# A two-layer transformer with a modulated conv and attention block on one core: five small moves in a hand-written order of work

## The chip, the core and the metric

The kernel runs on one core of a Trainium2 chip. The metric is the time of one execution in microseconds on the device (us). Before the change the median of three runs is 2548.13 us, from 2547.11 to 2549.5.

## What is computed

The input x has 256 positions of width 2048, all in float32. Two transformer layers come first, the first with stick-breaking attention, the second with latent attention; each ends in `residual_update`, where `x + rms_norm(out)` gets a gated term. Then one modulated block follows. Cut to what matters here:

```python
def residual_update(x, out, g_post, p_i, w_pp, w_pg):
    x = x + rms_norm(out, g_post)
    return x + (p_i @ w_pp) * jax.nn.sigmoid(x @ w_pg)
...
mod = silu(c) @ w_ada + b_ada                       # 2048 -> 6 * 2048
sh1, sc1, gt1, sh2, sc2, gt2 = split(mod, 6)
h = rms_norm_2(x, g_pre_mix) * (1.0 + sc1) + sh1
u_glu, q, k, v, qi, ki, wi, gates = split(h @ w_in)
y_conv = silu(layer_norm(depthwise_conv_31_taps(a * sigmoid(gt)))) @ w_conv_out
y_attn = top_64_attention(q, k, v, qi, ki, wi) @ w_attn_out
mixed = (g_conv * y_conv + g_attn * y_attn) @ w_o
x = x + gt1 * rms_norm_2(mixed, g_post_mix)
h = rms_norm_2(x, g_pre_ffn) * (1.0 + sc2) + sh2
x = x + gt2 * rms_norm_2((silu(h @ w_gate) * (h @ w_up)) @ w_down, g_post_ffn)
```

The convolution runs over 1024 channels with 31 taps each along the positions.

## The kernel before

**Products.** The 256 positions are two tiles t of 128. Each float32 product is made of three products of a high and a low part: for each 128 rows of a weight, L270 multiplies the left side's high part with the weight's high part wh, L271 the high part with the weight's low part wl, and L272 the low part with wh. The usual form is 128x512 (weight slices of 512 columns; 384 and smaller occur too).

**Units and blocks.** A block is one 512-wide column slice of a weight matrix, times both tiles. `Run.go` goes through the blocks in order. Its smallest step is a unit u: one tile t and one weight item i (two chunks of 128 rows for a 512-wide slice, so six matmuls). `self.u` counts the units, and everything else is placed by this counter when the program is written; the engines then run their instructions in that order, each engine for itself.

**Weights.** `pump` brings weights up to LEAD = 10 units ahead of use. `load` (L131) sends a transfer from the SP queue into a staging tile `wst`, of which there are STAGE = 4. `consume` makes wh with ACT (L148) and wl with DVE (L149) from it, into rings of RING = 6 tiles; weights with a gain use L153 and L154.

**Side work.** Whatever is not a main product is written as generators, which `side` advances once per unit; `yield n` means that the next step comes n units later. Those added by `add` are the urgent ones. `ensure` forces the generators that a product's left side still lacks. When tile 0 of a block with an `enter` function is written (a phase change), `go` first finishes all urgent generators and then calls `enter` (L277 to L280).

**Modulation.** The 6 x 2048 values of `mod` are made in 24 column pieces q of 512, each from 16 chunks k. A chunk is a transfer of 256 KB issued by POOL (L247) into a tile `ast` (XBUF = 3) and one DVE row (L416 for k = 0, otherwise L419), which adds it into `ada` with the value of silu(c) as the scalar. `spread` gives each chunk a unit; pieces 0 to 19 lie between unit 100 and unit uf − 60 (uf is the first FFN unit), without the surroundings of phase changes, and pause for the start of the modulated block. `side` writes either one chunk's DVE row or one chunk's transfer in a unit. After chunk 15, `ada_sum(q)` is added: a high part on ACT (L432), a low part on DVE (L433), two matmuls with a matrix of ones (L436, L437) that sum over the partitions, twice; a store to `mod`; and after each fourth piece a load back and a transpose on PE (L452). For `gt1` and `gt2` a row of gates is made and stored as well. `gain_of` (DVE) turns `sc` into the gain of a norm, and `begin_m` broadcasts the gate row at the phase change to w_o.

**Out projections.** After the output product of a layer, `to_gate` updates x (DVE L786) and transposes it (PE L370, called by `feed`), as the left side of the gate product. `feed` makes the transposed tile's high part (`ah`, ACT L381, or in its very first call DVE L379) and low part (`al`, DVE L383; without a scale DVE L375).

**Convolution.** `conv` makes one group of 128 channels: a first row (DVE L1234) and 30 rows (DVE L1237), which add one tap each on 128 partitions with up to 255 positions. After four rows or so it yields CONV_PACE units. `conv_chain` runs through channel groups 0 to 3 and 4 to 7, and then `conv_norm`. At the same time, DVE makes the scores and the top-64 selection of the attention (L1358 to L1375), and the weight splits.

ACT loads a table of functions (ACT_TABLE_LOAD) wherever its function is not in the loaded one.

Of the kernel before, what the change touches and what calls it, by code (L numbers as in the profile page):

```python
# [31 lines left out]
AHEAD_F = 3  # L32
LEAD_AHEAD = 20
LEAD_TURN = 6
CONV_PACE = 3
TO_C = ((2, 2, 2, (0, 2)), (2, 2, 2, (0, 2)))
TO_F = ((2, 2, 2, (0, 1, 2)), (2, 4, 2, (0, 1, 2)))
G_AT = (-1, -1, -1, 7)
# [51 lines left out]
class Run:  # L90
# [3 lines left out]
    def __init__(self, nc, main, psum, blocks, extra):  # L94
        self.nc, self.main, self.psum, self.blocks = nc, main, psum, blocks
        self.u = 0
        self.freed = 0
        self.urgent = []
        self.queue = deque()
        self.active = []  # L100
        self.width, self.space, self.last = 2, 4, -100
        self.items, self.need, u = [], [], 0
        for b in blocks:
            b.items = [{"p": len(self.items) + i, "b": b, "i": i} for i in range(b.np)]
            b.u0 = u
            first = {}
            for t, i in b.units():
                first.setdefault(i, u)
                u += 1
            self.items += b.items  # L110
            self.need += [first[i] for i in range(b.np)]
        self.ring = [0]
        for it in self.items:
            it["ahead"] = it["i"] < it["b"].n_ahead
            self.ring.append(self.ring[-1] + (not it["ahead"]))
        self.nextc = self.nextd = 0
        self.hooks = {}
        self.extra = extra(self) if extra else []
        self.xd = self.xc = 0
# [60 lines left out]
    def add(self, gen, act=None, t=None):  # L180
# [3 lines left out]
            act.gens[t].append(rec)  # L184
        return rec

    def back(self, gen, after=(), acts=()):
        rec = [gen, 0, False, after]
        self.queue.append(rec)
        for act, t in acts:  # L190
            act.gens[t].append(rec)
        return rec
# [34 lines left out]
    def side(self):  # L227
        for rec in list(self.urgent):
            if not rec[2] and rec[1] <= self.u:
                self.advance(rec)  # L230
        self.urgent = [r for r in self.urgent if not r[2]]
        self.active = [r for r in self.active if not r[2]]
        if (self.queue and len(self.active) < self.width and self.u >= self.last + self.space
                and all(r[2] for r in self.queue[0][3])):
            rec = self.queue.popleft()
            rec[1] = self.u
            self.active.append(rec)
            self.last = self.u
        self.step()
        if self.xc < self.xd and self.extra[self.xc][0] <= self.u:  # L240
            x = self.extra[self.xc]
            x[2](x[3])
            self.xc += 1
        elif (self.xd < len(self.extra) and self.xd - self.xc < XBUF and self.extra[self.xd][0] - 12 <= self.u):
            x = self.extra[self.xd]
            st = self.main.tile([P, NB], F32, tag="ast", bufs=XBUF, name="ast")
            self.nc.gpsimd.dma_start(st, x[1])  # L247
            x.append(st)
            self.xd += 1

    def go(self):
        nc = self.nc
        for b in self.blocks:
# [4 lines left out]
            for t, i in b.units():  # L258
                if t not in acc:
                    tag, bufs = ("sc", 2) if b.spare and t == 1 else ("acc", 3)  # L260
                    acc[t] = self.psum.tile([P, NB], F32, tag=tag, bufs=bufs, name=tag)
                it = b.items[i]
                self.ensure(act, t, b.cp * (i + 1))
                self.pump(it["p"])
                wh, wl = it["w"]
# [17 lines left out]
                    self.advance(rec)  # L283
                self.side()
                self.pump()
        while self.urgent or self.queue or self.active:
            self.u += 1
            self.side()

# [2 lines left out]
def body(ctx, tc, a, out):  # L292
# [68 lines left out]
        x.part = lambda t, g, m: tuple(y[:, g : g + m, sl(t)] for y in tiles())  # L361
        return x

    def feed(act, t, kc0, src, scale=None, first=False):


        m = src.shape[-1] // P
        tp = psum_t()
# [6 lines left out]
            nc.vector.tensor_sub(lo, v, hi.bitcast(F32))  # L375
        else:
            for c in range(m):
                if first:
                    nc.vector.tensor_scalar(hi[:, c, :], v[:, c, :], scale(kc0 + c), None, op0=ALU.mult)  # L379
                else:  # L380
                    nc.scalar.activation(hi[:, c, :], v[:, c, :], AF.Copy, scale=scale(kc0 + c))  # L381
            for c in range(m):
                nc.vector.scalar_tensor_tensor(lo[:, c, :], v[:, c, :], scale(kc0 + c), hi[:, c, :].bitcast(F32),  # L383
                                               op0=ALU.mult, op1=ALU.subtract)
# [24 lines left out]
    def ada_chunk(q, k):  # L409
        c0 = q * NB  # L410

        def use(w):
# [5 lines left out]
            acc = ada_acc[q]  # L418
            nc.vector.scalar_tensor_tensor(acc, w, s, acc, op0=ALU.mult, op1=ALU.add)  # L419
            if k == 15:  # L420
                run.add(ada_sum(q))

        return a["w_ada_2"][0, k * P : (k + 1) * P, c0 : c0 + NB], use

# [42 lines left out]
            yield 3  # L467
            st["gp"] = row_tile(gate_row(1))

    mod_rows, gate_rows = {}, {}  # L470

    def gate_row(n):
        return gate_rows[n].rearrange("(o k) p -> o (k p)", o=1)
# [1 line left out]
    def mod(i):  # L475
        return mods[:, 16 * i : 16 * i + 16]
# [53 lines left out]
    def begin_a():  # L530
# [47 lines left out]
        def prep():  # L578
            for g in range(4):
                for t in range(2):  # L580
                    feed(actA, t, 4 * g, x_nat[t][:, g * NB : (g + 1) * NB], lambda k: pre0[:, k : k + 1],
                         first=g == 0 and t == 0)
                    if g == 0 and t == 0:
                        warm(2)
                    yield PREP[2 * g + t]
# [252 lines left out]
    def layer_tail(layer, w_out, act_o, src, act_gate, act_next, then, last_groups=None):  # L838
# [13 lines left out]
                run.add(f(), act_p, t)  # L852

        def to_gate(t, r, update):
            yield 2
            xs = [update(0)]
            yield 1
            for g in range(4):
# [306 lines left out]

    def gain_of(i, name):

        nc.vector.scalar_tensor_tensor(gsc[:, i, :], mod(3 * i + 1), 1.0, cols[:, GC[name] : GC[name] + 16],
                                       op0=ALU.add, op1=ALU.mult)

# [365 lines left out]
        nc.scalar.activation(xo, xo, AF.Copy, accum_out=st["oss"][t][:, 4 + j : 5 + j])  # L1536

    def begin_m():
        st["gp"] = row_tile(gate_row(0))

    out_phase(a["w_o_2"][0], actM, begin_m, lambda t: spill[1][t], actF, to_f, mix_sums, last_groups=[1, 1, 6])
# [89 lines left out]
    def spread(run):  # L1631
# [3 lines left out]
        turns = [b.u0 for b in blocks if b.enter is not None or b.ahead is not None or b.w.tensor.name == a["w_ple_proj"].tensor.name]  # L1635
        xs = []
        uc = conv_block.u0
        for qs, us in ((range(20), calm(100, uc - 30) + calm(uc + 290, uf - 60)), (range(20, 24), calm(uf + 40, uf + 300))):
            todo = [(q, k) for q in qs for k in range(16)]
            for i, (q, k) in enumerate(todo):  # L1640
                xs.append([us[len(us) * i // len(todo)], *ada_chunk(q, k)])
# [53 lines left out]
```

## Time and profile before

| what | value |
|---|---|
| median of 3 runs | 2548.13 us (2547.11 to 2549.5) |
| profiled execution, its own time | 2550.05 us |
| span of the profile | 2548.3 us |
| mean clock granted to the matmuls in it | 0.992 |
| DMA | 562.49 MB, mean 221 GB/s |
| chain that ended last | PE 89%, DVE 4%, ACT 3%, DMA 2%, issue 1%, POOL 1% |

The span runs from the first to the last instruction of the profile; the execution's own time is 1.75 us longer. Engines are PE (matmul), PEld (its weight loads), DVE (vector), ACT (activation), POOL and SP. A row of a timeline shows the start, the duration, the engine, the line of the kernel, the operation, the output and inputs, the count and, in brackets, how long the engine was idle before and what ended that. Matmuls are pipelined: a 128x512 matmul has 0.39 us, but the next one starts earlier, so distances between starts are what counts. PEclk is the granted clock, 1.00 at full speed.

### The profile page before, as it was taken

Reading aid. Unit: us, or ns where it says so; the run is one execution under the profiler, and the core shown is the slowest. Engines: PE = TensorE matmul, PEld = TensorE weight load, DVE = VectorE, ACT = ScalarE, POOL = GpSimd, SP = SyncE. Lnnn points to the kernel's source line nnn. Section 1 sums busy time; section 2 is a strip of 40 time slices with the busy share of each in tenths; the row PEclk is TensorE's granted clock in tenths of the full one; section 3 lists DMA queues with packets and bytes.
Section 4 is the critical chain, followed back from the end, with each engine's and each line's share of the span. In section 5 each row is a group of like instructions: output and inputs, shape, how many; then the busy total and the mean of one; then the engine's idle time right before and its main releaser. Section 6 shows DMA issues by size and latency. Waiting matters only on the chain.

```text
span 2548.3 us, 33086 instructions
## 1 busy us (share of the span) xinstructions
PE 2489.3 (98%) x11904; PEld 2066.6 (81%) x11904; DVE 1708.6 (67%) x2349; ACT 1298.0 (51%) x1915; POOL 298.2 (12%) x561
## 2 busy tenths in 40 slices
PE   9999999999999999999999999989999999999998
PEld 7888888778888777878877878877788888888886
DVE  5466677777865577667998857775765566655545
ACT  6655564556656545554544564445544444444443
POOL 2011112211324321000000001110110010000000
PEclk9999999999999999999999999999999999999999
DMA  7577778877885496665647547884577777676563
GB/s 243 177 235 254 254 229 304 276 231 251 286 256 169 156 325 225 220 201 177 189 141 209 176 135 256 288 281 164 184 240 235 238 236 235 219 236 189 190 193 125
DMA packets 272212, 562.49 MB, mean 221 GB/s; under 512 B 20985, under 2 KB 43929, under 8 KB 270001
## 3 DMA queue, kind: packets, MB, share of 16 engines
q1 hardware_dynamic: 236688, 438.56, 54.5%
q0 software_dynamic: 34448, 120.67, 13.7%
q8 instruction: 93, 1.52, 0.2%
q10 hardware_dynamic: 912, 1.17, 0.1%
q14 instruction: 71, 0.57, 0.1%
HBM read 551.86 MB, written 8.45 MB: 220 GB/s over the span
## 4 chain that ended last, share of the span: by engine, by line
PE 89%; DVE 4%; ACT 3%; DMA 2%; issue 1%; POOL 1%; DVEq 0%; SPq 0%; ACTq 0%; POOLq 0%
PE acc L270 20%; PE acc L272 20%; PE acc L271 20%; PE sc L270 7%; PE sc L272 7%; PE sc L271 7%; DVE wl L149 1%; PE sc L1049 1%; PE tp L370 1%; ACT wh L148 1%; PE pv L1049 1%; DMA ast<-in_w_ada_dram 1%; DMA wst<-in_w_o_dram 0%; PE sc L677 0%; DVE cv L1237 0%
## 5 line engine op out<-in xcount | busy, mean ns | idle before, releaser
L149 DVE TENSOR_TENSOR wl<-wst,wh 128x1024 fp32r<-128x1024 f32 (+3 forms) x794 | 948.8, 1199 | 578.8 <-ACT wh L148 576.5
L148 ACT ACTIVATE wh<-wst 128x1024 fp32r<-128x1024 f32 (+3 forms) x794 | 822.3, 1039 | 829.8 <-PE sc L272 421.9
L270 PE MATMUL acc<-wh,ah 128*128 128x512 f32 (+4 forms) x1918 | 752.1, 392 | 3.0 <-ACT wide L1441 3.0
L271 PE MATMUL acc<-wl,ah 128*128 128x512 f32 (+4 forms) x1918 | 738.9, 385 | 1.5 <-DVE wl L149 1.5
L272 PE MATMUL acc<-wh,al 128*128 128x512 f32 (+4 forms) x1918 | 738.4, 385 | 0.9 <-DVE al L375 0.9
L270 PEld LDWEIGHTS acc<-wh,ah 128*128 128x128 f32 x1918 | 362.6, 189 | 72.4 <-ACT wide L1441 3.4
L272 PEld LDWEIGHTS acc<-wh,al 128*128 128x128 f32 x1918 | 361.9, 189 | 72.6 <-DVE al L375 1.4
L271 PEld LDWEIGHTS acc<-wl,ah 128*128 128x128 f32 x1918 | 362.7, 189 | 67.7 <-DVE wl L149 3.3
L247 POOL DMA_DIRECT2D ast<-in_w_ada_dram x384 | 209.1, 545 | 1553.8 <-DVE ada L419 1298.0
L419 DVE SCALAR_TENSOR_TENSOR ada<-ast,silu_c,ada 128x512 f32<-128x512 f32 x360 | 269.5, 749 | 60.1 <-DMA ast<-in_w_ada_dram 59.6
L270 PE MATMUL sc<-wh,ah 128*128 128x512 f32 x554 | 218.8, 395 | 0.0
L271 PE MATMUL sc<-wl,ah 128*128 128x512 f32 x554 | 216.9, 391 | 0.0
L272 PE MATMUL sc<-wh,al 128*128 128x512 f32 x554 | 216.8, 391 | 0.0
L272 PEld LDWEIGHTS sc<-wh,al 128*128 128x128 f32 x554 | 104.7, 189 | 22.3
L271 PEld LDWEIGHTS sc<-wl,ah 128*128 128x128 f32 x554 | 104.8, 189 | 21.2
L270 PEld LDWEIGHTS sc<-wh,ah 128*128 128x128 f32 x554 | 104.5, 189 | 21.0
L1237 DVE SCALAR_TENSOR_TENSOR cv<-cv,wdw 128x255 f32<-128x255 f32 (+14 forms) x240 | 112.3, 468 | 6.5
L153 ACT ACTIVATE wh<-wst,cols 128x512 fp32r<-128x512 f32 (+2 forms) x112 | 68.3, 666 | 33.3 <-PE acc L272 20.1
L154 DVE SCALAR_TENSOR_TENSOR wl<-wst,cols,wh 128x512 fp32r<-128x512 f32 (+2 forms) x112 | 71.7, 684 | 17.7 <-ACT wh L153 17.5
L270 PE MATMUL sc<-wh,hh 128*128 128x512 f32 x176 | 68.9, 392 | 0.0
L270 PE MATMUL acc<-wh,hh 128*128 128x512 f32 x176 | 68.9, 391 | 0.0
L272 PE MATMUL sc<-wh,hl 128*128 128x512 f32 x176 | 68.6, 390 | 0.0
(377 smaller groups left out, 2887.0 us busy)
## 6 DMA issues: line engine op xcount, KB each, us to landing
ast<-in_w_ada_dram POOLq DMA_DIRECT2D x384, 256.0 KB, 4.3
wst<-in_w_in_dram SPq DMA_DIRECT2D x144, 512.0 KB
wst<-in_w_in_a_dram SPq DMA_DIRECT2D x120, 512.0 KB
wst<-in_w_gate_dram SPq DMA_DIRECT2D x88, 512.0 KB
wst<-in_w_up_dram SPq DMA_DIRECT2D x88, 512.0 KB
wst<-in_w_down_dram SPq DMA_DIRECT2D x88, 512.0 KB
wst<-in_w_ple_gate_dram SPq DMA_DIRECT2D x64, 512.0 KB
wst<-in_w_in_b_dram SPq DMA_DIRECT2D x40, 512.0 KB
```

The source lines that it names most:

```text
L148: nc.scalar.activation(wh, st, AF.Copy)
L149: nc.vector.tensor_sub(wl, st, wh.bitcast(F32))
L153: nc.scalar.activation(wh[:, c, :], st[:, c, :], AF.Copy, scale=g)
L154: nc.vector.scalar_tensor_tensor(wl[:, c, :], st[:, c, :], g, wh[:, c, :].bitcast(F32), op0=ALU.mult, op1=ALU.subtract)
L247: self.nc.gpsimd.dma_start(st, x[1])
L270: nc.tensor.matmul(o, lhsT=hi, rhs=wh[:, c, :], start=kc == 0, stop=False)
L271: nc.tensor.matmul(o, lhsT=hi, rhs=wl[:, c, :], start=False, stop=False)
L272: nc.tensor.matmul(o, lhsT=lo, rhs=wh[:, c, :], start=False, stop=kc == b.cp * b.np - 1)
L370: nc.tensor.transpose(tp[:, c * P : (c + 1) * P], src[:, c * P : (c + 1) * P], ident)
L419: nc.vector.scalar_tensor_tensor(acc, w, s, acc, op0=ALU.mult, op1=ALU.add)
L1049: nc.tensor.matmul(o, lhsT=l, rhs=r, start=start, stop=True, skip_group_check=True)
L1237: nc.vector.scalar_tensor_tensor(acc[:, sft:], u[:, : S - sft], wdw[:, c, k : k + 1], acc[:, sft:], op0=ALU.mult, op1=ALU.add)
```

## The change

It has five parts.

1. `ada_sum` is no longer an urgent generator but goes on a list `slow`, which `side` advances after the urgent ones and which a phase change does not finish. `ready` finishes the sums that a user needs, in `gain_of` and `begin_m`. Pieces 0 to 19 are spread up to unit uf − 110 instead of uf − 60.
2. `to_gate` waits four units instead of two before its first update, in both layers.
3. In the first block, the weights of a unit are pumped ahead of the generators for its left side.
4. The first feed no longer makes its high parts on DVE; all are made on ACT.
5. CONV_PACE is 2 instead of 3.

```diff
-CONV_PACE = 3
+CONV_PACE = 2
...
+    def later(self, gen):
+
+        rec = [gen, self.u + 1, False]
+        self.slow.append(rec)
+        return rec
...
-        self.urgent = [r for r in self.urgent if not r[2]]
-        self.active = [r for r in self.active if not r[2]]
+        for rec in self.slow:
+            if rec[1] <= self.u:
+                self.advance(rec)
+        self.urgent, self.slow, self.active = ([r for r in x if not r[2]] for x in (self.urgent, self.slow, self.active))
...
                 it = b.items[i]
+                if b is self.blocks[0]:
+                    self.pump(it["p"])
                 self.ensure(act, t, b.cp * (i + 1))
                 self.pump(it["p"])
...
-                if first:
-                    nc.vector.tensor_scalar(hi[:, c, :], v[:, c, :], scale(kc0 + c), None, op0=ALU.mult)
-                else:
-                    nc.scalar.activation(hi[:, c, :], v[:, c, :], AF.Copy, scale=scale(kc0 + c))
+                nc.scalar.activation(hi[:, c, :], v[:, c, :], AF.Copy, scale=scale(kc0 + c))
...
-                run.add(ada_sum(q))
+                ada_done.setdefault(q // 4, []).append(run.later(ada_sum(q)))
...
+    def ready(*vectors):
+        for i in vectors:
+            for rec in ada_done[i]:
+                run.finish(rec)
...
         def to_gate(t, r, update):
-            yield 2
+            yield 4
...
     def gain_of(i, name):
+        ready(3 * i, 3 * i + 1)
...
     def begin_m():
+        ready(2)
         st["gp"] = row_tile(gate_row(0))
...
-calm(uc + 290, uf - 60)
+calm(uc + 290, uf - 110)
```

The order of the instructions on the engines shows where they come to stand. Line numbers of the changed kernel are some 6 to 12 higher: L280 to L282 are its three products, L1248 its conv row, L1386 its end of the selection. First DVE, behind the end of the top-64 selection (`sel`), where the convolution (`cv`) of the kernel before begins its sixth group of channels:

```order
L1375 TENSOR_SCALAR sel<-score 128x384
L149 TENSOR_TENSOR wl<-wst,wh 128x1024
L1234 TENSOR_SCALAR cv<-cv,wdw,cols 128x256
L1237 SCALAR_TENSOR_TENSOR cv<-cv,wdw 128x255
L1237 SCALAR_TENSOR_TENSOR cv<-cv,wdw 128x254
L149 TENSOR_TENSOR wl<-wst,wh 128x1024
L1237 SCALAR_TENSOR_TENSOR cv<-cv,wdw 128x253
L1237 SCALAR_TENSOR_TENSOR cv<-cv,wdw 128x252
L1237 SCALAR_TENSOR_TENSOR cv<-cv,wdw 128x251
L1237 SCALAR_TENSOR_TENSOR cv<-cv,wdw 128x250
L149 TENSOR_TENSOR wl<-wst,wh 128x1024 x2
```

The same place of the changed kernel, where the eighth and last group is half done:

```order
L1386 TENSOR_SCALAR sel<-score 128x384
L149 TENSOR_TENSOR wl<-wst,wh 128x1024
L1248 SCALAR_TENSOR_TENSOR cv<-cv,wdw 128x241
L1248 SCALAR_TENSOR_TENSOR cv<-cv,wdw 128x240
L1248 SCALAR_TENSOR_TENSOR cv<-cv,wdw 128x239
L1248 SCALAR_TENSOR_TENSOR cv<-cv,wdw 128x238
L149 TENSOR_TENSOR wl<-wst,wh 128x1024
L1248 SCALAR_TENSOR_TENSOR cv<-cv,wdw 128x237
L1248 SCALAR_TENSOR_TENSOR cv<-cv,wdw 128x236
L1248 SCALAR_TENSOR_TENSOR cv<-cv,wdw 128x235
L1248 SCALAR_TENSOR_TENSOR cv<-cv,wdw 128x234
L149 TENSOR_TENSOR wl<-wst,wh 128x1024
```

Before, 6 channel groups have been begun at this place; now all 8, so more conv rows stand ahead of the same weight split, and four of them lie between any two splits.

PE at the phase change to w_o before, with the sums' matmuls (`adh`, `adl`, `ada`) between two products:

```order
L270 MATMUL acc<-wh,ah 128x512
L271 MATMUL acc<-wl,ah 128x512
L272 MATMUL acc<-wh,al 128x512
L436 MATMUL tp<-adh,ones_r 128x256
L437 MATMUL tp<-adl,ones_r 128x256
L436 MATMUL tp<-adh,ones_r 128x256
L437 MATMUL tp<-adl,ones_r 128x256
L452 MATMUL tp<-ident,ada 128x16
L270 MATMUL sc<-wh,ah 128x512
```

PE of the changed kernel where its last transpose of these sums stands, about a hundred matmuls earlier:

```order
L280 MATMUL acc<-wh,cv 128x512
L281 MATMUL acc<-wl,cv 128x512
L282 MATMUL acc<-wh,cv 128x512
L458 MATMUL tp<-ident,ada 128x16
L280 MATMUL acc<-wh,cv 128x512
L281 MATMUL acc<-wl,cv 128x512
```

The transpose, and with it the four matmuls ahead of it, have left the phase change and stand among the product before w_o.

ACT at the start of the program before (`wh` the weights' high parts, `ah` those of the first feeds):

```order
L148 ACT_TABLE_LOAD
L148 ACTIVATE wh<-wst 128x512 x4
L381 ACTIVATE ah<-tp,pre_77 128x128 x8
L148 ACTIVATE wh<-wst 128x512 x3
L381 ACTIVATE ah<-tp,pre_77 128x128 x4
```

And in the changed kernel:

```order
L148 ACT_TABLE_LOAD
L148 ACTIVATE wh<-wst 128x512 x4
L387 ACTIVATE ah<-tp,pre_77 128x128 x12
L148 ACTIVATE wh<-wst 128x512 x3
L387 ACTIVATE ah<-tp,pre_77 128x128 x4
```

Four high parts have come from DVE to ACT, behind the first four weight copies.

More of the change, by code (lines that the diff above doesn't have):

```diff
@@ L97, in __init__ @@
         self.freed = 0
-        self.urgent = []
+        self.urgent, self.slow = [], []
         self.queue = deque()
@@ L285, in go @@
                 self.pump()
-        while self.urgent or self.queue or self.active:
+        while self.urgent or self.queue or self.active or self.slow:
             self.u += 1
@@ L362, in pair_act, with feed @@
         return x
-    def feed(act, t, kc0, src, scale=None, first=False):
+    def feed(act, t, kc0, src, scale=None):
         m = src.shape[-1] // P
@@ L468, in ada_sum @@
             st["gp"] = row_tile(gate_row(1))
-    mod_rows, gate_rows = {}, {}
+    mod_rows, gate_rows, ada_done = {}, {}, {}
+    def ready(*vectors):
+        for i in vectors:
+            for rec in ada_done[i]:
+                run.finish(rec)
     def gate_row(n):
@@ L580, in prep @@
                 for t in range(2):
-                    feed(actA, t, 4 * g, x_nat[t][:, g * NB : (g + 1) * NB], lambda k: pre0[:, k : k + 1],
-                         first=g == 0 and t == 0)
+                    feed(actA, t, 4 * g, x_nat[t][:, g * NB : (g + 1) * NB], lambda k: pre0[:, k : k + 1])
                     if g == 0 and t == 0:
@@ L1637, in spread @@
         uc = conv_block.u0
-        for qs, us in ((range(20), calm(100, uc - 30) + calm(uc + 290, uf - 60)), (range(20, 24), calm(uf + 40, uf + 300))):
+        for qs, us in ((range(20), calm(100, uc - 30) + calm(uc + 290, uf - 110)), (range(20, 24), calm(uf + 40, uf + 300))):
             todo = [(q, k) for q in qs for k in range(16)]
```

## The prediction

> **What bounds the kernel now.** I read the page first, then the waits of PE, then busy time stretch by stretch where the diff touches something, then timelines of the single waits.
>
> ```profile
> span 2548.3 us, 33086 instructions
> ...
> PE 2489.3 (98%) x11904; PEld 2066.6 (81%) x11904; DVE 1708.6 (67%) x2349; ACT 1298.0 (51%) x1915; POOL 298.2 (12%) x561
> ```
>
> PE is busy for 98% of the span. An edit can shorten the run only by PE's waits and slow-clock stretches, and lengthens it wherever it makes PE wait. The waits of PE name the places (us in total, times, longest):
>
> ```profile
> PE tp L370 <- DVE x L786: 6.1, 6, 2.0
> PE tp L452 <- DMA ada<-mod: 4.1, 1, 4.1
> PE tp L436 <- ACT adh L432: 3.7, 3, 2.2
> ...
> PE acc L270 <- ACT wide L1441: 3.0, 1, 3.0
> ...
> PE tp L370 <- issue: 2.5, 1, 2.5
> PE tp L437 <- DVE adl L433: 2.5, 3, 0.9
> PE acc L271 <- DVE wl L149: 1.5, 1, 1.5
> ```
>
> L436, L437 and L452 are the modulation sums (10.3 us together), L370 the transposes after the residual update. DVE's weight split L149 stops PE once, at the start. Now the busy time of all engines, in the convolution, just after it, in the w_o phase change and behind it, and in two pieces of layer 0's residual update (columns: PE, PEld, DVE, ACT, POOL, then the granted clock and DMA):
>
> ```profile
> 1158.00:1344.00 186.00, 186.00 (x943) 158.41 (x943) 168.50 (x322) 85.83 (x118) 0.00 (x0) 1.00 0.57 168
> 1349.00:1356.00 7.00, 6.95 (x19) 5.47 (x20) 6.79 (x12) 2.60 (x4) 0.00 (x0) 0.58 0.71 220
> 1722.00:1729.00 7.00, 6.96 (x21) 5.59 (x22) 2.85 (x5) 4.43 (x11) 0.00 (x0) 0.65 0.00 1
> 503.00:507.00 4.00, 2.66 (x14) 1.82 (x12) 4.00 (x6) 2.36 (x4) 0.00 (x0) 1.00 0.73 251
> 516.00:520.00 4.00, 2.00 (x12) 1.41 (x11) 2.87 (x4) 2.03 (x3) 0.54 (x1) 1.00 0.78 257
> ```
>
> In the 186 us from 1158 to 1344 PE never waits, but DVE has only 186 − 168.5 = 17.5 us of idle time. Elsewhere DVE has room (67% over the span); there it has not. What fills it, the groups of DVE in that stretch:
>
> ```profile
> L1237 DVE SCALAR_TENSOR_TENSOR cv<-cv,wdw 128x255 f32<-128x255 f32 (+9 forms) x164 | 76.9, 469 | 4.5
> L149 DVE TENSOR_TENSOR wl<-wst,wh 128x1024 fp32r<-128x1024 f32 (+2 forms) x67 | 73.9, 1113 | 12.3 <-ACT wh L148 12.2
> ...
> L1234 DVE TENSOR_SCALAR cv<-cv,wdw,cols 128x256 f32<-128x256 f32 x6 | 2.4, 407 | 0.0
> ```
>
> **The denser conv steps.** The convolution is 8 channel groups of 31 rows, 248 DVE rows in all. Before, 164 + 6 = 170 of them lie ahead of 1344 us. With a pace of 2 units instead of 3, the order of the changed kernel puts all 248 ahead of the weight split that stands at 1342.45 here. That split is already just in time (DVE, then PE, then the two ACT groups that PE waits for):
>
> ```profile
> 1342.45 2.35 DVE L149 TENSOR_TENSOR wl<-wst,wh 128x1024 fp32r<-128x1024 f32 x2
> ```
>
> ```profile
> 1344.54 0.39 PE L270 MATMUL acc<-wh,ah 128*128 128x512 f32 x1
> ...
> 1349.05 0.79 PE L270 MATMUL acc<-wh,ah 128*128 128x512 f32 x1 [2.99 <-ACT wide L1441]
> ...
> 1355.06 0.40 PE L272 MATMUL acc<-wh,al 128*128 128x512 f32 x1
> ```
>
> ```profile
> 1347.46 1.06 ACT L148 ACTIVATE wh<-wst 128x1024 fp32r<-128x1024 f32 x1 [2.01 <-DMA wst<-in_w_in_dram]
> 1348.42 1.06 ACT L1441 ACTIVATE wide<-acc 128x512 f32<-128x512 f32 x2
> ```
>
> The first half of the x2 group ends near 1343.7, and the unit that needs it starts at 1344.54: 0.9 us of slack. DVE is in order, so 248 − 170 = 78 more rows at 0.469 us, 36.6 us, stand in front of it. If all 17.5 us of idle time and the slack absorb what they can, PE waits 36.6 − 17.5 − 0.9 = 18.2 us. If the idle time before L149, 12.3 us of waiting for ACT's half, cannot be filled, it is 18.2 + 12.3 = 30.5 us. The fuller DVE is, the less it waits for ACT, so I take a value near the lower end, 21 us. Spread over many units, this should leave the clock alone: from 503 to 507 and from 516 to 520 PE was busy for 66% and 50% of the time at a clock of 1.00. The wait of 2.99 us at 1349.05 was, however, followed by slow matmuls (clock 0.58): the 14 steps from 1349.05 to 1355.06 took 6.01 us, and at 0.227 us each would take 3.2, so 2.8 us went there. Is that stall of 2.99 + 2.8 = 5.8 us still there afterwards? ACT's L1441 stands behind a weight copy that waits for a transfer into a staging tile, and that tile comes free only with a DVE split four items earlier. DVE will be as late then as now, so I leave the stall in; it may go (−5.8), or a second cold stretch may come (+2.8). Conv stage: +21, from 18.2 − 5.8 = +12.4 to 30.5 + 2.8 = +33. After it DVE is freer than before, which returns nothing, as PE does not wait for DVE there.
>
> On the clock the Trainium skill (TensorE: Matmul & The Clock Gate, Part 1: The HAM clock gate) says that the gate watches free-running windows of about 3.4 us and throttles after an idle one. The wait of 2.99 us is shorter and was followed by 0.58 all the same, so the trace bears the rule out only roughly; by the page alone no second cold stretch could come from waits like these, and the upper end would be 30.5 instead of 33.
>
> The order also puts 23 table loads on ACT instead of 18, since exponentials and sigmoids now alternate. A load took 1.28 us:
>
> ```profile
> L1025 ACT ACT_TABLE_LOAD x2 | 2.6, 1283 | 0.0
> ```
>
> Five are 6.4 us. ACT is idle for 100 of the 186 us, so I cost them at nothing; all of them on the path would be +6.4, part of my upper side. The Trainium skill (ScalarE: Activation LUTs, What ACT_TABLE_LOAD costs) adds a drain and gives 2.66 us a switch: an estimate of 13.3 us, which that idle time would hold too.
>
> **Modulation sums that nobody waits for.** PE at the w_o phase change, then at the earlier one:
>
> ```profile
> 1711.13 0.39 PE L271 MATMUL acc<-wl,ah 128*128 128x512 f32 x1
> 1711.36 0.39 PE L272 MATMUL acc<-wh,al 128*128 128x512 f32 x1
> 1712.43 0.38 PE L436 MATMUL tp<-adh,ones_r 128*128 128x256 f32 x1 [0.69 <-ACT adh L432]
> ...
> 1722.05 0.26 PE L452 MATMUL tp<-ident,ada 16*128 16x16 f32 x1 [4.12 <-DMA ada<-mod]
> 1722.23 0.80 PE L270 MATMUL sc<-wh,ah 128*128 128x512 f32 x1
> ...
> 1726.66 0.52 PE L271 MATMUL acc<-wl,ah 128*128 128x512 f32 x1
> ```
>
> ```profile
> 919.32 0.39 PE L272 MATMUL acc<-wh,al 128*128 128x512 f32 x1
> ...
> 922.25 0.39 PE L436 MATMUL tp<-adh,ones_r 128*128 128x256 f32 x1 [0.77 <-ACT adh L432]
> ...
> 922.93 0.40 PE L270 MATMUL acc<-wh,ah 128*128 128x512 f32 x1
> ```
>
> Matmuls start 0.227 us apart (1711.13, 1711.36), so the product could go on at 1711.59; it does at 1722.23, 10.6 us later. The five small matmuls move into the stream and keep some 0.7 us. The 11 steps from 1722.23 to 1726.66 take 4.43 us instead of 2.50: 1.9 more. Saved: 10.6 − 0.7 + 1.9 ≈ 12 us. At the earlier one 922.93 − 919.55 = 3.4, less 0.5 of moved work: 2.9 us. In the new order the last transpose of the sums stands in the product before w_o, about a hundred matmuls ahead, so no guard finds one undone. The gate row's broadcast still starts at this phase change; it is used only by the block's output, so it is covered. Ends: −16 and −10.
>
> **Transposes two units later.** In both layers PE waits at L370 for DVE's residual update, the 6.1 us above, and 2.5 us put down to issue: 8.6 us at most can go. But DVE itself is late there, and partly for a transfer:
>
> ```profile
> 502.25 0.75 DVE L419 SCALAR_TENSOR_TENSOR ada<-ast,silu_c,ada 128x512 f32<-128x512 f32 x1 [1.73 <-DMA ast<-in_w_ada_dram]
> ...
> 517.13 0.75 DVE L419 SCALAR_TENSOR_TENSOR ada<-ast,silu_c,ada 128x512 f32<-128x512 f32 x1 [1.43 <-DMA ast<-in_w_ada_dram]
> ```
>
> ```profile
> 987.88 0.75 DVE L419 SCALAR_TENSOR_TENSOR ada<-ast,silu_c,ada 128x512 f32<-128x512 f32 x1 [3.94 <-DMA ast<-in_w_ada_dram]
> ```
>
> Update and transposes move together, and ending the chunk stream 50 units earlier makes chunks denser, so some more L419 rows (0.66 us apart) come between. I take −1, between −8.6 and +4 (six rows more).
>
> **The start.** The hi halves of the first feed move from DVE, idle then, to ACT behind four weight copies:
>
> ```profile
> 6.28 1.12 DVE L379 TENSOR_SCALAR ah<-tp,pre 128x128 fp32r<-128x128 f32 x4 [2.74 <-PE tp L370]
> ...
> 9.28 0.63 ACT L148 ACTIVATE wh<-wst 128x512 fp32r<-128x512 f32 x1 [0.89 <-DMA wst<-in_w_in_a_dram]
> ...
> 9.68 0.63 PE L272 MATMUL acc<-wh,al 128*128 128x512 f32 x1
> ```
>
> ACT is through with the copies at 9.9 and each half then needs 0.3 us on ACT and as much on DVE, so the first L272 comes near 11 instead of 9.68: +1.5, between 0 (the weights' transfers are late next) and +3 (all four halves in the chain).
>
> **Sum**, on the profiled run's 2550.05 us: + 21 − 12 − 2.9 − 1 + 1.5 = + 6.6, so 2556.7. The median of the runs shown, 2548.13, is 1.9 below the profiled run: 2554.8, rounded to 2555.0.
>
> **Rivals.** All times are against the median; a difference of 0.2%, 5.1 us, is about what a measurement of this kernel can tell from none, so the bounds are 2543.0 and 2553.2.
> - *DVE's lead swallows the conv rows* (faster): DVE splits weights up to ten units ahead of PE (60 matmuls at 0.227, 13.6 us at most), and that lead comes on top of the idle time. Once both together hold more than 30 of the 36.6 us, the conv stage costs 4 us or so, the other terms (−12 − 2.9 − 1 + 1.5 = −14.4) win, and the time is 2548.1 + 4 − 14.4 ≈ 2538. Against it: the lead was there before too, and was used up by 1342. 0.10; and 0.04 for a conv stage at +12 with transposes at −5: 2542.
> - *Gains and losses meet* (same): the conv stage at its low end, +12.4, as the old stall goes: 2548.1 + 12.4 − 14.4 ≈ 2546. For it speaks DVE's lighter load behind the convolution; against it, that the staging tile still waits for a late split. Up to 2553 with the ends between: 0.26.
> - *The phase change still waits* (slower): something else is late next, such as the weights behind it, and the 12 us stay: 2567. No wait for weights shows at 1722.23, which speaks against it. 0.08.
> - My forecast, with its upper side up to +33 in the conv stage (2567): 0.52.
>
> Faster 0.14, same 0.26, slower 0.60. The range 2542 to 2567 leaves out the first rival and the top of the conv stage.
>
> **What would show it.** Right: PE waits on the weight split (wl) from about the fifth to the eighth conv channel, 18 us or more in all; no wait at the sums' matmuls; the product running on through the w_o phase change at full clock. Wrong: PE without waits up to the end of the selection, or DVE with idle time left in that stretch; a wait of the same size at w_o with another releaser; a transpose wait gone altogether.

## The result, and the profile after

The changed kernel takes 2580.58 us (median of 4 runs, 2579.65 to 2580.95), the kernel before beside it 2548.74 us. The ratio is 1.0125, with an interval from 1.011 to 1.014: 32 us slower, where 7 us slower were forecast, and outside of the range. The profiled execution took 2580.69 us.

First the page of the changed kernel, its span and the busy times of the engines:

```profile
span 2578.8 us, 33119 instructions
...
PE 2493.4 (97%) x11904; PEld 2067.5 (80%) x11904; DVE 1709.0 (66%) x2345; ACT 1305.8 (51%) x1924; POOL 290.5 (11%) x561
```

The work is almost the same as before on every engine (DVE 1709.0 us beside 1708.6; ACT has 7.8 us more, most of it for five more table loads), so the 30.5 us that the span grew are waits and slow matmuls of PE. Its waits (us in total, times, longest):

```profile
PE pv L1274 <- DVE nat L1271: 12.7, 1, 12.7
PE tp L379 <- DVE x L796: 6.5, 9, 1.4
...
PE acc L281 <- DVE wl L149: 4.9, 5, 3.3
PE tp L663 <- ACT nat L654: 4.5, 2, 3.6
PE acc L280 <- ACT qkv L675: 4.0, 1, 4.0
...
PE tp L1005 <- POOL qr L936: 2.8, 3, 2.3
```

The sums' waits for their transfer (L452 before, 4.1 us) are gone. In their place a single wait of 12.7 us stands on top, at a matmul of the convolution's norm that had waited 0.4 us before. To see where the time went, it helps to compare when the same unit starts in both traces: the first of the unit's products, by its start in the timeline of PE. The last column is how late the changed kernel is there.

| unit | what begins or lies here | before | after | after − before |
|---|---|---|---|---|
| 2 | start | 12.10 | 14.48 | 2.4 |
| 330 | ahead of layer 0's residual update | 495.98 | 498.19 | 2.2 |
| 450 | latent layer, projections | 669.78 | 672.12 | 2.3 |
| 455 | | 676.69 | 681.89 | 5.2 |
| 530 | latent attention | 795.87 | 805.81 | 9.9 |
| 592 | behind the earlier phase change | 924.30 | 929.48 | 5.2 |
| 743 | modulated block begins | 1149.84 | 1157.64 | 7.8 |
| 876 | conv steps nearly over | 1327.95 | 1355.36 | 27.4 |
| 879 | conv norm | 1332.18 | 1377.97 | 45.8 |
| 892 | | 1355.98 | 1398.20 | 42.2 |
| 1000 | | 1529.71 | 1573.17 | 43.5 |
| 1126 | last unit ahead of the w_o phase change's wait | 1710.23 | 1754.15 | 43.9 |
| 1129 | behind it | 1727.26 | 1758.23 | 31.0 |
| 1703 | last unit | 2534.12 | 2564.69 | 30.6 |

So three steps make all but 0.1 of the 30.6: + 7.8 up to the modulated block, + 35.7 in the convolution and the attention beside it (743 to 1000), − 13.0 at the w_o phase change.

Each position is read from one execution, and two executions of the same instructions differ. Up to unit 743 the kernel of experiment 3 has the program of the kernel before, and is 3.7 us late there; experiments 1 and 2 have that of the changed kernel, and are 6.8 and 10.4 us late beside its 7.8. So a difference of up to some 4 us ahead of unit 743 says little by itself.

**The convolution.** Busy times of all engines (PE, PEld, DVE, ACT, POOL, clock, DMA) in the changed kernel, up to the end of the selection and from there to the norm:

```profile
1168.00:1364.00 196.00, 179.91 (x882) 149.35 (x880) 189.08 (x381) 79.45 (x113) 0.00 (x0) 0.98 0.49 145
1364.00:1378.00 14.00, 1.54 (x5) 1.27 (x5) 13.15 (x21) 2.11 (x2) 0.00 (x0) 0.50 0.61 184
```

DVE's idle time has fallen from 17.5 us to 6.9 (196 − 189.08), while PE, which never waited here, lacks 16 us, and then 12.5 of 14. DVE's groups in the first of the two stretches:

```profile
L1248 DVE SCALAR_TENSOR_TENSOR cv<-cv,wdw 128x255 f32<-128x255 f32 (+14 forms) x228 | 106.9, 469 | 6.2
L149 DVE TENSOR_TENSOR wl<-wst,wh 128x1024 fp32r<-128x1024 f32 (+2 forms) x60 | 65.9, 1099 | 0.1
...
L1245 DVE TENSOR_SCALAR cv<-cv,wdw,cols 128x256 f32<-128x256 f32 x8 | 3.3, 408 | 0.0
```

A conv row takes 469 ns as before; there are now 236 of them, and DVE no longer waits for ACT's half of a weight (0.1 us ahead of L149, before 12.3): PE's weights have become the late ones. PE, and then DVE, at the norm:

```profile
1358.64 0.39 PE L280 MATMUL acc<-wh,ah 128*128 128x512 f32 x1
1362.34 0.50 PE L281 MATMUL acc<-wl,ah 128*128 128x512 f32 x1 [3.31 <-DVE wl L149]
...
1363.37 0.40 PE L282 MATMUL acc<-wh,al 128*128 128x512 f32 x1
1376.46 2.07 PE L1274 MATMUL pv<-nat,mean_c 128*128 128x256 f32 x4 [12.69 <-DVE nat L1271]
1377.97 0.99 PE L280 MATMUL acc<-wh,ah 128*128 128x512 f32 x1
```

```profile
1361.07 1.22 DVE L149 TENSOR_TENSOR wl<-wst,wh 128x1024 fp32r<-128x1024 f32 x1
1362.20 1.97 DVE L1248 SCALAR_TENSOR_TENSOR cv<-cv,wdw 128x241 f32<-128x241 f32 x4
1364.09 1.22 DVE L149 TENSOR_TENSOR wl<-wst,wh 128x1024 fp32r<-128x1024 f32 x1
...
1371.22 1.92 DVE L1248 SCALAR_TENSOR_TENSOR cv<-cv,wdw 128x229 f32<-128x229 f32 x4
1373.12 1.23 DVE L149 TENSOR_TENSOR wl<-wst,wh 128x1024 fp32r<-128x1024 f32 x1
1374.27 0.68 DVE L1269 TENSOR_TENSOR nat<-cv 128x512 f32<-128x512 f32 x1
1374.98 1.42 DVE L1271 TENSOR_TENSOR nat<-nat,cv 128x512 f32<-128x512 f32 x2
```

DVE works without a gap from 1361 to 1376. The split that PE's wait of 3.31 us ends with (1361.07) belongs to the unit at hand; behind it DVE's queue holds four more splits, for eight units to come, with conv rows between, and only then the norm's sums L1269 and L1271. PE's queue has the norm's matmul right behind the unit at hand. So PE waits until DVE has worked off its lead, although the weights that come out of it meanwhile are ready to be multiplied.

**The w_o phase change.** PE in the changed kernel at the place where the kernel before stood for 10.6 us:

```profile
1755.28 0.39 PE L282 MATMUL acc<-wh,al 128*128 128x512 f32 x1
1755.51 0.39 PE L280 MATMUL sc<-wh,ah 128*128 128x512 f32 x1
```

The product goes on, at 0.23 us a step and a clock of 1.00. What comes ahead of unit 743 is seen best in the experiments.

### The profile page after: what moved, and what is told of

Its sections match the earlier page's. It is cut to its first block, busy times and chain, and to the rows that moved or that the text cites. A ratio compares the mean times of both kernels' runs of the same rounds, so it can differ in the third digit from the quotient of the medians.

```text
span 2578.8 us, 33119 instructions
## 1 busy us (share of the span) xinstructions
PE 2493.4 (97%) x11904; PEld 2067.5 (80%) x11904; DVE 1709.0 (66%) x2345; ACT 1305.8 (51%) x1924; POOL 290.5 (11%) x561
## 4 chain that ended last, share of the span: by engine, by line
PE 82%; DVE 9%; ACT 3%; issue 2%; DMA 2%; POOL 1%; SPq 0%; DVEq 0%; POOLq 0%; ACTq 0%
PE acc L280 18%; PE acc L282 18%; PE acc L281 18%; PE sc L280 7%; PE sc L282 7%; PE sc L281 7%; DVE wl L149 3%; DVE cv L1248 3%; PE tp L379 1%; PE sc L1059 1%; DMA ast<-in_w_ada_dram 1%; PE pv L1059 1%; ACT wh L148 1%; PE sc L687 0%; DVE wl L154 0%
## 5 line engine op out<-in xcount | busy, mean ns | idle before, releaser
L149 DVE TENSOR_TENSOR wl<-wst,wh 128x1024 fp32r<-128x1024 f32 (+3 forms) x794 | 950.8, 1200 | 607.4 <-ACT wh L148 605.4
L280 PE MATMUL acc<-wh,ah 128*128 128x512 f32 (+4 forms) x1918 | 753.6, 393 | 8.0 <-ACT qkv L675 4.0
L282 PE MATMUL acc<-wh,al 128*128 128x512 f32 (+4 forms) x1918 | 739.7, 386 | 0.4 <-DVE al L384 0.4
L280 PEld LDWEIGHTS acc<-wh,ah 128*128 128x128 f32 x1918 | 363.0, 189 | 77.8 <-ACT qkv L675 4.5
L282 PEld LDWEIGHTS acc<-wh,al 128*128 128x128 f32 x1918 | 362.4, 189 | 72.7 <-DVE al L384 0.8
L280 PE MATMUL sc<-wh,ah 128*128 128x512 f32 x554 | 217.4, 392 | 0.0
L282 PE MATMUL sc<-wh,al 128*128 128x512 f32 x554 | 215.7, 389 | 0.0
L282 PEld LDWEIGHTS sc<-wh,al 128*128 128x128 f32 x554 | 104.0, 188 | 21.9
L280 PEld LDWEIGHTS sc<-wh,ah 128*128 128x128 f32 x554 | 104.0, 188 | 20.9
L1248 DVE SCALAR_TENSOR_TENSOR cv<-cv,wdw 128x255 f32<-128x255 f32 (+14 forms) x240 | 112.4, 468 | 6.5
L280 PE MATMUL sc<-wh,hh 128*128 128x512 f32 x176 | 68.9, 392 | 0.0
L280 PE MATMUL acc<-wh,hh 128*128 128x512 f32 x176 | 68.9, 391 | 0.0
L282 PE MATMUL sc<-wh,hl 128*128 128x512 f32 x176 | 68.6, 390 | 0.0
```

Of the source, the lines that this page charges most:

```text
L149: nc.vector.tensor_sub(wl, st, wh.bitcast(F32))
L280: nc.tensor.matmul(o, lhsT=hi, rhs=wh[:, c, :], start=kc == 0, stop=False)
L282: nc.tensor.matmul(o, lhsT=lo, rhs=wh[:, c, :], start=False, stop=kc == b.cp * b.np - 1)
L1248: nc.vector.scalar_tensor_tensor(acc[:, sft:], u[:, : S - sft], wdw[:, c, k : k + 1], acc[:, sft:], op0=ALU.mult, op1=ALU.add)
```

## The experiments

All comparisons are with the kernel before, timed beside each of them; ratios carry the interval. Its median in those runs was between 2550.4 and 2551.1 us.

**1. The conv steps back to a pace of 3.**

```diff
-CONV_PACE = 2
+CONV_PACE = 3
```

> The changed kernel with CONV_PACE back at 3, all else kept. Theory A, the conv steps alone cost what the changed kernel loses between units 749 and 1000 (its lag behind the kernel before grows there from 7.8 to 43.5 us, so 35.7): the time falls by about 36 us, to 2543 to 2547, PE's wait of 12.7 us at the conv norm's matmul is gone. Rival B, a good part of the 35.7 comes from the modulation work that was moved into or out of that stage: the time stays above 2555.

2543.07 us, ratio 0.9972 (0.9961 to 0.9983): 37 to 39 us less than the changed kernel (by the times, by the ratios), and faster than the kernel before. Theory A held. The lag is 6.8 us at unit 743 and 5.6 at unit 1000, so without the denser steps nothing is lost there; at the end it is −7.4.

**2. The conv norm later.** In the changed kernel:

```diff
         acc = st["cacc"]
-        yield 1
+        yield 14
         mu = psum_v()
```

> The changed kernel with the conv norm's first step 14 units after the end of the conv steps instead of 1. Theory A, the wait of 12.7 us comes from the order of DVE's queue (the norm's sums stand behind weight splits made up to ten units ahead, and PE's matmul stands at its own unit, so DVE's whole lead has to be made good there): the wait goes, about 12 us fall away, 2566 to 2570; some 20 us of waits on the weight split stay. Rival B, DVE has simply too much work, and PE will wait as long for the weight splits instead: 2578 to 2582.

2575.56 us, ratio 1.0094 (1.0079 to 1.011). 5 to 8 us less than the changed kernel (by the times, by the ratios), not 12: neither number was met. The waits of PE from unit 870 to 890:

```profile
1364.90 0.50 PE L281 MATMUL acc<-wl,ah 128*128 128x512 f32 x1 [3.32 <-DVE wl L149]
1384.45 0.50 PE L280 MATMUL acc<-wh,ah 128*128 128x512 f32 x1 [2.92 <-ACT wide L1452]
1390.57 1.13 PE L1274 MATMUL pv<-nat,mean_c 128*128 128x256 f32 x4 [1.73 <-DVE nat L1271]
```

The wait of 12.7 us is gone, 1.7 are left of it. At unit 888 this kernel has lost 25.1 us since unit 743 (from 10.4 to 35.5), the changed one 39.5 (from 7.8 to 47.3). So the mechanism of A is right: 14 us were the order of DVE's queue at the norm. But the changed kernel gets 5 back at once (47.3 at unit 888, 42.2 at 892), as the old stall at L1452 does not occur in it; here it does. My reading, not tried by itself, is that DVE fills its lead during the long wait. The rest goes later: from unit 892 to 1000 this kernel loses 5.0, the changed one 1.3. The selected attention, which waits for the end of the norm, begins later.

**3. The conv steps alone.** The kernel before, with

```diff
-CONV_PACE = 3
+CONV_PACE = 2
```

> The kernel before with CONV_PACE 2 alone. Theory A, the conv steps cost the 35.7 us by themselves: 2582 to 2587. Rival B, they need the moved modulation work to cost that much: below 2575, near 2569 if my forecast's 21 us were right for the pace alone.

2587.76 us, ratio 1.0143 (1.0129 to 1.0157), 37 us slower. Theory A held, 0.8 us above its range: from unit 743 to 1000 this kernel loses 35.8 us (from 3.7 to 39.5), what the changed kernel loses (35.7). The other edits have no part in it that shows.

**4. Pace 3, and the chunks' end as before.**

```diff
-CONV_PACE = 2
+CONV_PACE = 3
...
-calm(uc + 290, uf - 110)
+calm(uc + 290, uf - 60)
```

> The changed kernel with CONV_PACE 3, and the modulation chunks spread up to uf - 60 again instead of uf - 110. Before unit 743 the changed kernel is 7.8 us late, 2.3 of them from the start, where I had expected a gain. Theory A, the denser and shifted chunks cost this (they meet the rotations on POOL and the updates on DVE at worse places): about 6 to 8 us less than with uf - 110, 2536 to 2540. Rival B, it is the sums' matmuls, which now stand inside running stages and wait for DVE and ACT there: within 2 us of the kernel with uf - 110, 2543 to 2547.

2538.19 us, ratio 0.9948 (0.9935 to 0.996), 5 us less than with uf − 110, and −2.5 at unit 743 instead of 6.8, a gain of 9.3. Theory A, for the first part of the program. The trace is that of this kernel's fastest execution (2535.16 us, 3.0 below the median), so the 9.3 are rather too much.

**5. The slow list alone.** The kernel before, with

```diff
-                run.add(ada_sum(q))
+                ada_done.setdefault(q // 4, []).append(run.later(ada_sum(q)))
```

and what belongs to it (`later`, `slow` in `side`, `ready`).

> The kernel before with the slow list and its guards alone (chunks up to uf - 60, transposes, start and conv pace as before). Theory A, this is the change's only gain: the waits at units 591 and 1127 go (3.4 and 13 us in the changed kernel), so about 14 to 17 us less, 2532 to 2536 beside 2549 to 2551. Rival B, the sums that now stand inside running stages take 4 us or more of it back: 2537 to 2541.

2537.61 us, ratio 0.9953 (0.994 to 0.9965). 12 us less, at the near end of rival B. Up to unit 743 it is 0.5 us early, with 3.4 us gained at unit 591 and about 3 lost around it. The time is rival B's. But 1.3 of those 3 us are lost in experiment 3 too (units 592 to 743), which changes nothing there, so it isn't shown that the sums inside the stages take them back. At unit 1129 it is 14.9 early, and 2.5 of that are gone by unit 1174.

**6. The chunks' end alone.** The kernel before, with

```diff
-calm(uc + 290, uf - 60)
+calm(uc + 290, uf - 110)
```

> The kernel before with the chunks spread up to uf - 110 alone; the sums stay urgent. Theory A, the denser and shifted chunks cost some 9 us ahead of unit 743 by themselves, and the last sum is through before the w_o phase change, which then waits for nothing (13 us): 2543 to 2548, later than the kernel before by 7 to 9 us at unit 743. Rival B, they cost only together with sums inside the stages: 2535 to 2539, with less than 3 us of lag at unit 743.

2549.32 us, ratio 0.9997 (0.9988 to 1.0006). The edit pays for itself and no more: 15.5 us late at unit 743 (about 12 by the medians, as the trace is that of the slowest of eleven executions, 2552.91), and 13.0 back at the w_o phase change, where the last sum is through in time although nothing else was done to it. So it is A's mechanism, with a larger loss than A had; neither time was met. Here are PE's waits over the whole run and, for 480 to 560 us around layer 0's residual update, DVE's rows for the chunks, first those of the kernel before, then those of this one:

```profile
PE tp L370 <- DVE x L786: 11.5, 10, 3.0
...
PE tp L1058 <- DVE mods L453: 3.5, 1, 3.5
...
PE tp L436 <- DVE cql L383: 2.6, 1, 2.6
```

```profile
L419 DVE SCALAR_TENSOR_TENSOR ada<-ast,silu_c,ada 128x512 f32<-128x512 f32 x14 | 10.5, 747 | 4.0 <-DMA ast<-in_w_ada_dram 3.9
```

```profile
L419 DVE SCALAR_TENSOR_TENSOR ada<-ast,silu_c,ada 128x512 f32<-128x512 f32 x21 | 15.7, 746 | 5.9 <-DMA ast<-in_w_ada_dram 5.9
```

Seven rows more stand in a place where PE waits for DVE anyway. These are the surroundings of a phase change, which `spread` leaves free. Why chunks are there is seen in the program: `side` writes a chunk's DVE row or a chunk's transfer, one of the two in a unit, so half a chunk per unit at most. The plan asks for 0.64 before (101 chunks from unit 100 to 258) and for 0.68 with uf − 110 (109 from 100 to 259). The rest is written late, up to unit 338 before and up to 356 now, and in the next stretch up to 637 and 650.

**7. The later transposes alone.** The kernel before, with

```diff
         def to_gate(t, r, update):
-            yield 2
+            yield 4
```

> The kernel before with the residual update and its transposes two units later, alone. Theory A, DVE is the late one there and moves with it: within 2 us of the kernel before. Rival B, the two units are what DVE lacked, and the L370 waits go: 5 to 8 us less.

2550.3 us, ratio 0.9999 (0.999 to 1.0007). Theory A: the waits at L370 for DVE's update and those put down to issue add to 8.5 us, before to 8.6.

**8. Fewer conv rows during the selection.** The kernel before, with the slow list, the later transposes and

```diff
-                yield CONV_PACE
+                yield 4 if 820 <= run.u < 890 else CONV_PACE
```

> The kernel before with the slow list, the later transposes, and conv steps every 4 units instead of 3 between units 820 and 890 (the top-64 selection), every 3 elsewhere; the start as before. Theory A, DVE's lack of time in that stretch is also what makes the old stall of 5.8 us (a wait of 3.0 us and slow matmuls) at unit 890: with some 24 conv rows fewer ahead of it, 11 us of DVE time, the stall goes: 2527 to 2532. Rival B, the stall comes from the transfers into the staging tiles, whatever DVE does: it stays, 2533 to 2537.

2535.81 us, ratio 0.9944 (0.9932 to 0.9957), beside 0.9953 and 0.9948 for the kernels with pace 3: unclear by the time. At the place itself A held. PE's wait at the old stall:

```profile
1347.73 0.50 PE L278 MATMUL acc<-wh,ah 128*128 128x512 f32 x1 [0.90 <-ACT wide L1455]
```

0.9 us instead of 3.0, and no slow matmuls behind it; between units 888 and 892 this kernel gains 4.8 us, the ones with pace 3 some 1.5. By unit 1060 it has given back 3.2 of it, as the selected attention begins later. At the stall this is the opposite of the change and goes the opposite way; over the whole run the times don't tell a gain from none.

**9. The chunks on their plan, end at uf − 110.** The kernel of experiment 6, with

```diff
-        elif (self.xd < len(self.extra) and ...
+        if (self.xd < len(self.extra) and ...
```

> The kernel before with the chunks up to uf - 110 and side() writing a chunk's DVE row and a chunk's transfer in the same unit where both are due (if instead of elif). As it was, one of the two per unit meant half a chunk per unit at most, while the plan asks for 0.69 (109 chunks in units 100 to 259); the rest was written later, up to unit 356 and 648, inside the surroundings of the phase changes that the plan leaves free. Theory A, this overrun is what costs 15.5 us ahead of unit 743 with uf - 110 alone: the chunks now end at 323, 395, 563, 626 as planned, the lag at unit 743 falls below 6 us, and the time to 2535 to 2541. Rival B, it is the denser stream in the stages itself: no better than 2549, more likely worse.

2530.05 us, ratio 0.9921 (0.9908 to 0.9935): 19 us less than without this edit, better than A had it, and rival B is out. At unit 743 it is 7.8 us early instead of 15.5 late. The row of the chunks from 480 to 560 us:

```profile
L419 DVE SCALAR_TENSOR_TENSOR ada<-ast,silu_c,ada 128x512 f32<-128x512 f32 x10 | 7.5, 747 | 1.7 <-DMA ast<-in_w_ada_dram 1.6
```

10 instead of 21, and none of them between 494 and 535, where the transposes are. L370 no longer waits for DVE at all. A part of the gain goes elsewhere, as the first wait of this kernel shows:

```profile
PE tp L995 <- POOL qr L926: 10.2, 9, 2.0
```

**10. The chunks on their plan, with the slow list and uf − 60.** The kernel of experiment 5 with the same `if`.

> The kernel before with the slow list (chunks up to uf - 60) and the same edit to side(), so that the chunks keep to the plan (0.64 per unit from 100 to 258). Theory A, the overrun, from 322 to 338 and from 563 to 597 here, still costs some of the L370 waits (3.6 and 2.6 us with the slow list): 2 to 5 us less than the slow list alone, 2532 to 2536. Rival B, density in the stages takes as much back: 2537 to 2541.

2528.77 us, ratio 0.9914 (0.9901 to 0.9928): 9 us less than the slow list alone. Theory A, with more than it gave. It is 9.3 us early at unit 743. Its first wait:

```profile
PE tp L1008 <- POOL qr L939: 6.8, 8, 1.7
```

**11. The chunks from unit 60 on, with the slow list.** The kernel of experiment 5, with

```diff
-calm(100, uc - 30)
+calm(60, uc - 30)
```

> The kernel before with the slow list (chunks up to uf - 60), the chunks from unit 60 on instead of 100; one step per unit as before. The stream is thinner (0.58 planned per unit) and runs over its stretches by less (to 328 instead of 338, and to 583 instead of 637). Theory A, as above: 2 to 5 us less than the slow list alone, 2532 to 2536. Rival B, nothing is gained where DVE has room anyway: 2536 to 2539.

2530.76 us, ratio 0.9921 (0.9907 to 0.9934). Theory A again, and more: 7.8 us early at unit 743, by a thinner stream instead of a faster one.

**12. Both.** The kernel of experiment 10, chunks from unit 60 on.

> The kernel before with the slow list, the chunks on plan as in the run before, and from unit 60 on. With the chunks on plan PE now waits for POOL's rotations (6.8 us, 8 times) between units 500 and 560, where the chunks' transfers stand ahead of them on POOL: 8 us of the gain go back there. Theory A, what counts there is the number of chunks per unit, and starting at 60 makes them fewer (0.58 instead of 0.64): 1 to 3 us less than on plan from unit 100, 2525 to 2528. Rival B, the rotations wait as long for any chunk ahead of them: 2528 to 2531.

2533.44 us, ratio 0.9933 (0.992 to 0.9947). A is out; even B was too good. From unit 500 to 560 it loses 10.1 us, the kernel of experiment 10 loses 7.8, and its waits for the rotations are again 6.8 us:

```profile
PE tp L1008 <- POOL qr L939: 6.8, 6, 1.8
```

A thinner stream doesn't help there. It is also behind the other by 2.3 us at unit 300 and 3.3 at unit 455, and why stays open; the intervals of experiments 10 and 12 overlap.

The lowest median is that of experiment 10: 2528.77 us, 0.9914 of the kernel before. It has of the change only the slow list with its guards, and one word of its own. Experiments 9 and 11, both at 0.9921, can't be told from it by their intervals; so with the chunks on their plan the earlier end alone does as well, and the slow list on top of the plan isn't shown to be needed.

## Why the prediction was wrong

The direction was right, and for its main reason, but two terms of the sum were wrong, both by more than their ends.

| term | forecast | measured | where |
|---|---|---|---|
| conv stage | +21 (12.4 to 33) | +35.7; alone +35.8 | units 743 to 1000, experiment 3 |
| w_o phase change | −12 | −13.0 | units 1126 to 1129 |
| earlier phase change | −2.9 | −3.4 | units 590 to 592 |
| transposes two units later | −1 | about 0 | experiment 7 |
| start | +1.5 | +2.4 | unit 2 |
| denser chunks ahead of unit 743 | nothing of their own, up to +4 with the transposes | +9.3 by the traces, 5 to 6 by times and ratios | experiments 1 and 4 |

**The conv stage.** The count of rows was right, and their duration. The step that failed is "PE waits 36.6 − 17.5 − 0.9 = 18.2 us". It measured the lateness at one weight split, that of unit 888, as if weight splits were the only thing PE takes from DVE. But PE also takes the norm's sums, and they are queued on DVE behind splits for units to come. At the end of the conv steps PE therefore pays DVE's lead as well: 12.7 us of waiting at L1274. In experiment 2, where the norm stands 14 units later, the loss at unit 888 is 25.1 us, and the sum of the forecast then comes out if DVE's real idle time, that of the changed kernel, is put in: 36.6 − 0.9 − (17.5 − 6.9) = 25.1. That it fits to the decimal is luck. Taking 21 for it was 4 us too little, as DVE kept 6.9 us of idle time where I let it keep about 3: 6.2 of the 6.9 stand ahead of conv rows, 0.027 us a row, and the 4.5 us ahead of the 164 rows before were the same 0.027 each. Such idle time grows with the rows and can't take them in, so it should have been counted with their price. The other 14 us are the norm's wait. The norm was in the code and in the order of the instructions, two lines below the conv steps; in the trace of before it showed nothing, because the chain ended there in a stretch with time to spare: PE waited 0.4 us for it.

The way by which a late DVE stops PE was not the forecast one either. The sign was to be 18 us or more of waits on the weight split. The changed kernel has 4.9 us of them; 4.5 and 4.0 us are put down to ACT's rows L654 and L675. Here is the second of these waits, ACT first, then PE:

```profile
1347.93 1.06 ACT L148 ACTIVATE wh<-wst 128x1024 fp32r<-128x1024 f32 x1 [4.65 <-DMA wst<-in_w_in_dram]
1348.90 1.07 ACT L675 ACTIVATE qkv<-acc 128x512 f32<-128x512 f32 x2
```

```profile
1349.53 0.50 PE L280 MATMUL acc<-wh,ah 128*128 128x512 f32 x1 [4.02 <-ACT qkv L675]
...
1350.42 0.63 PE L280 MATMUL acc<-wh,ah 128*128 128x512 f32 x1
1350.84 0.63 PE L281 MATMUL acc<-wl,ah 128*128 128x512 f32 x1
```

ACT's row stands behind a weight copy that waits for its transfer, and the transfer needs a staging tile that DVE frees; in the trace every wait of the SP queue in this stretch (1168 to 1376 us) is put down to DVE. It is the pattern of the old stall, now at two more places, and slow matmuls follow (0.43 us a step), where the prediction had the clock left alone.

The old stall of 5.8 us was left in the sum; with the norm early it does go, with the norm late it stays, and with fewer conv rows (experiment 8) it shrinks. So it depends on how late DVE is, as the working had it.

**The chunks.** "ending the chunk stream 50 units earlier makes chunks denser, so some more L419 rows (0.66 us apart) come between" had the right direction, and a price of six rows at most. There were 7 rows more at layer 0's update (12 instead of 5 between 494 and 535 us), but the larger part came elsewhere: 2.9 us between units 450 and 455 and 4.4 between 520 and 530, where the sums of the shifted pieces fell on matmuls of the latent layer. Experiments 1, 2 and 6, which end the chunks at uf − 110 too, lose 2.8 to 4.5 us and 5.2 to 8.0 us at these two places; experiment 4, with the slow list and uf − 60, loses nothing there. So it comes with the earlier end and not with the slow list. The rows of the changed kernel:

```profile
678.83 0.36 PE L442 MATMUL tp<-adh,ones_r 128*128 128x256 f32 x1 [2.35 <-DVE cql L389]
...
794.73 0.33 PE L1005 MATMUL tp<-ident,qr 128*128 128x128 f32 x1 [2.27 <-POOL qr L936]
...
799.58 0.44 PE L977 MATMUL tp<-ident,nat 128*128 128x128 f32 x2 [1.68 <-DVE mods L459]
```

The first and the third are a sum's own step and one queued behind it; at the second, POOL's rotations stand behind a chunk's transfer (what the transfer waited for in the 2.61 us ahead of it, the profile doesn't show):

```profile
792.54 0.58 POOL L255 DMA_DIRECT2D ast<-in_w_ada_dram  x1 [2.61 <-issue]
793.14 0.47 POOL L933 TENSOR_TENSOR qr<-nat,ropes 128x128 f32<-128x128 f32 x1
...
794.23 0.45 POOL L936 TENSOR_TENSOR qr<-qr,rm 128x128 f32<-128x128 f32 x1
```

I had looked at the edit where it ends, near unit 1121, and not along the 900 units over which it moves every chunk and sum. What the overrun costs is shown by experiment 9, which takes it away; as every late chunk and every sum behind it then stands earlier, it doesn't separate the rows in the gaps from the places where the sums fall. That the sums at these three places are the cause of the 7.3 us there is read from the rows, not tried by itself.

**The phase changes** came out as worked. But experiment 6 shows that the slow list was not needed for the larger one: with the last chunk 37 units earlier, the sum is through before unit 1127. Two parts of the change removed the same wait, so it could only be won once, and one of the two cost 5 to 15 us elsewhere (experiments 4 and 6).

**The table loads.** The trace after has 23, as the order had it. On ACT where the gate products and the first pairs of the selected attention now alternate:

```profile
1415.79 1.28 ACT L1452 ACT_TABLE_LOAD   x1
1417.08 0.60 ACT L1452 ACTIVATE wide<-acc 128x512 f32<-128x512 f32 x1
1417.68 1.28 ACT L1035 ACT_TABLE_LOAD   x1
1418.98 0.37 ACT L1035 ACTIVATE p<-sc,mx 128x128 f32<-128x128 f32 x1
```

A switch costs 1.29 to 1.30 us from the load to the next activation here. Two of them stand ahead of the p that PE waits for at 1419.94 (2.60 us, where the kernel before waited 0.7 at the same matmul). "Nothing" was nearly right: the stretch from unit 892 to 1000 loses 1.3 us in all. The Trainium skill (ScalarE: Activation LUTs, What ACT_TABLE_LOAD costs) has 2.66 us a switch with a drain; no such drain shows between these rows.

## What to carry over

When work on an in-order engine is made denser, look for every consumer of that engine, not only for the steady one: an occasional consumer that stands right behind the dense work in program order has to wait for all that was queued in advance of it, here four weight splits with conv rows between, 14 us. A stream that is spread by a plan should be checked against the rate at which it can be written: at half a chunk per unit against a plan of 0.64, the backlog ran into the gaps that the plan kept free, and one `if` for `elif` was worth 9 to 19 us, beside some 16 us for the two phase changes together. And where two edits remove the same wait, try each alone; the cheaper one is enough.

## What the runs showed of the hardware

Waits of about 3 us of PE were followed by slow matmuls in some cases and not in others. After 3.00 us in experiment 1 the steps took 0.43 us:

```profile
1355.90 0.79 PE L280 MATMUL acc<-wh,ah 128*128 128x512 f32 x1 [3.00 <-ACT wide L1452]
1356.49 0.63 PE L281 MATMUL acc<-wl,ah 128*128 128x512 f32 x1
1356.92 0.63 PE L282 MATMUL acc<-wh,al 128*128 128x512 f32 x1
```

At the same matmul they took 0.23 us after 2.92 us in experiment 2 (at 1384.45, shown there), and so did the 128x512 matmuls behind the wait of 3.00 us at L370 in experiment 6 (at 522.42). After the 3.32 us in experiment 2, which end at 1364.90, they took 0.23 us at first and 0.43 us only from 1366.42 on, for 3 us:

```profile
1366.42 0.63 PE L281 MATMUL acc<-wl,ah 128*128 128x512 f32 x1
1366.84 0.63 PE L282 MATMUL acc<-wh,al 128*128 128x512 f32 x1
```

After the 12.69 us of the changed kernel the matmuls were slow for some 4.5 us. So the length of a wait alone does not decide at about 3 us. The Trainium skill (TensorE: Matmul & The Clock Gate, Part 1: The HAM clock gate) calls the gate's window free-running, which would make it a matter of where the wait falls; no run here shows the window itself.
